# A decoder block in split float32 on one core: pool offsets, first gate/up weights, early form loads, two output queues

## The chip, the cores and the metric

The kernel runs on one core of one Trainium2 chip. The metric is the time of one execution in device microseconds (us), the median of repeated runs. A profile is one further execution with the hardware profiler on; its own time is given beside its span, since the two differ a little. PE is TensorE, DVE is VectorE, ACT is ScalarE, POOL is GpSimd, SP is SyncE; PEld is the load of the stationary operand on TensorE.

## The reference, cut to what matters

One decoder layer over 512 tokens of width 2048, everything in float32:

```
h   = RMSNorm(x)
[qA|kA|vA|qB|kB|vB|gA|gB] = h @ W_in
yA  = sliding-window attention (16 query heads, 4 key heads, window 128, sinks) @ W_branch_a
yB  = stick-breaking attention (16 heads, strictly causal) @ W_branch_b
x   = x + (sigmoid(gA) * yA + sigmoid(gB) * yB) @ W_out
x   = x + (silu(gate) * up) @ W_down      with [gate|up] = RMSNorm(x) @ W_ffn_in, 5632 wide
out = RMSNorm_final(x)
```

## The kernel before

**Products.** A float32 product is made of three passes over numbers that are rounded to the engine's fast 32-bit type: each operand is split in a high and a low part, and high*high, high*low and low*high are added in PSUM. Weights come in pieces of 128x1024: SP issues the load, ACT writes the high part (`whi`, line 153), DVE the low part (`wlo`, line 154). There are three buffers each of `raw`, `whi` and `wlo`, and the class `Weights` splits at most three pieces ahead of their use (`AHEAD`, line 128; `fill`, line 161). The list `todo` holds what is to be split; a callable in it stands for a piece of the feed-forward part, and `fill` stops at one as long as the pool `fp` doesn't exist.

**Stages.** First the input projection (lines 336 to 360 and 451 to 453), with both attentions worked off in between as pieces (`later`, `gap`); then the two branch projections, whose moving operands are `yh` and `yl`; then W_out (`rows`, lines 848 to 860; stationary operands `mh`, `ml`); then gate/up; then down.

**Gate/up and down.** Both use seven products in place of eight for a 2x2 block of sub-matrices (Strassen's scheme in Winograd's form): `p1` to `p7`, each on a sum of input quarters (a *form*, made by `make_forms`, lines 279 to 304) and a sum of weight quarters (`plan_group`, lines 210 to 246). One product step takes one pair of weight pieces with two forms and is 12 matmuls of 128x512 (`product`, lines 248 to 259). In these stages the form is the stationary operand (`fx`) and the weights (`whi`, `wlo`) move. `steps` (lines 200 to 208) sets the order of the steps: two products run in a staggered way, the second two steps behind the first, and at equal place the first one is ahead. There are 11 gate/up groups of 4 steps per product (each product reads the forms of pairs 0 to 7, two in a step), and 4 parts of down with 3, 3, 3 and 2 steps, each with two groups. In gate/up a `p5` piece is the sum of the `p1` piece (buffer `wx`) and a fresh load (`raw`); `p2` loads into the buffer `wz` that `p7` held.

**Forms between the stages.** Gate/up writes its results as forms to HBM (line 990, on POOL's queue); `load_forms` (lines 1012 to 1027) brings them back for down, on the same queue, together with the residual `x2`. Before the change it is called when the last gate/up group has been recorded. Even pairs land in pool `fp`, odd ones in pool `tp`. A DMA on POOL's queue that has to wait for a free tile holds up all that stand behind it.

**The end.** `finish` (line 1029) scales four tiles of 128 tokens by their root mean square, two column blocks on DVE and two on ACT, and SP issues the 16 stores of 256 KB (line 1039). The square root needs a table load on ACT.

**Order.** Instructions are recorded in the order of the code, and a scheduler then orders each engine's queue by its own model of times; dependencies through tiles and pools become waits.

**Places in SBUF.** From the left come the constants (`cp`), the weight buffers (`wp`) and 47 tiles of 2048 bytes (`tp`); from the right a pad of 24 numbers, 32 tiles of 2048 bytes (`ep`: `fh`, `fl`, `mh`, `ml`) and some constants (`ca`). Where `ep` and `ca` were, gate/up opens `fp` (21 tiles of 2048 bytes for `fx`, four each of 4096 bytes for `wx` and `wz`). In the program as built all tiles of `wp` and `tp` begin 512 bytes past a multiple of 2048 (`tp` at bytes 55,808 to 150,016 of a partition), and all of `ep` and `fp` begin 1920 bytes past one (`ep` at 163,712 to 227,200, `fp` from 153,472). `yh` and `yl` lie in `tp`; of the forms in gate/up pairs 0 to 4 lie in `tp` and 5 to 7 in `fp`.

## Time and profile before

| | us |
|---|---|
| median of 3 runs (2547.82 to 2552.52) | 2548.81 |
| the profiled execution's own time | 2547.38 |
| its span, first to last instruction | 2545.4 |

The page of the profile gives the busy time of each engine and the span in 40 slices (63.6 us each); the answers of the trace give single waits, single instructions with their start, and busy time by stretches. A matmul's duration in the trace is longer than the distance to the next one, since matmuls overlap in the array: how fast the engine goes is read from the starts, or from the number of matmuls in a stretch without a gap.

### The profile page before, as it was taken

Reading aid. Unit: us, or ns where it says so; the run is one execution under the profiler, and the core shown is the slowest. Engines: PE = TensorE matmul, PEld = TensorE weight load, DVE = VectorE, ACT = ScalarE, POOL = GpSimd, SP = SyncE. Lnnn points to the kernel's source line nnn. Section 1 sums busy time; section 2 is a strip of 40 time slices with the busy share of each in tenths; the row PEclk is TensorE's granted clock in tenths of the full one; section 3 lists DMA queues with packets and bytes.
Section 4 is the critical chain, followed back from the end, with each engine's and each line's share of the span. In section 5 each row is a group of like instructions: output and inputs, shape, how many; then the busy total and the mean of one; then the engine's idle time right before and its main releaser. Section 6 shows DMA issues by size and latency. Waiting matters only on the chain.

```text
span 2545.4 us, 33168 instructions
## 1 busy us (share of the span) xinstructions
PE 2502.8 (98%) x11529; PEld 2065.6 (81%) x11529; DVE 1980.7 (78%) x3457; ACT 1377.4 (54%) x2626; POOL 251.4 (10%) x482
## 2 busy tenths in 40 slices
PE   9999999999999999999999999999999999999997
PEld 8888878888887788888788888888888877888886
DVE  5688888888769644375788788888888877888888
ACT  6567777667657533265554555544555544333335
POOL 0000001111101000000010011100111024302100
PEclk9999999999999999999999999999999999999999
DMA  5232333333323644344456655566555689958652
GB/s 174 91 100 92 100 108 100 96 96 104 109 89 97 201 147 149 128 162 133 148 168 193 181 180 180 171 186 183 182 173 182 188 259 324 351 159 272 183 184 88
DMA packets 256295, 407.99 MB, mean 160 GB/s; under 512 B 16480, under 2 KB 103552, under 8 KB 256128
## 3 DMA queue, kind: packets, MB, share of 16 engines
q1 hardware_dynamic: 202096, 304.13, 38.5%
q0 software_dynamic: 46912, 89.15, 11.3%
q10 hardware_dynamic: 7120, 12.61, 1.3%
q8 instruction: 90, 1.47, 0.2%
q14 instruction: 77, 0.63, 0.1%
HBM read 344.48 MB, written 61.34 MB: 159 GB/s over the span
## 4 chain that ended last, share of the span: by engine, by line
PE 63%; issue 2%; ACT 1%; POOL 0%; DVE 0%; DMA 0%; ACTq 0%; POOLq 0%; DVEq 0%
PE mm L256 9%; PE mm L258 9%; PE mm L257 9%; PE at L256 7%; PE at L258 7%; PE at L257 7%; PE mm L341 3%; PE mm L342 3%; PE mm L340 3%; PE mm L856 1%; PE mm L857 1%; PE mm L858 1%; PE at L856 1%; PE at L858 1%; PE at L857 1%
## 5 line engine op out<-in xcount | busy, mean ns | idle before, releaser
L153 ACT CAST whi<-wx 128x1024 fp32r<-128x1024 f32 x264 | 277.2, 1050 | 333.5 <-PE at L258 150.5
L257 PE MATMUL mm<-wlo,fx 128*128 128x512 f32 x1056 | 417.3, 395 | 0.5 <-DVE wlo L154 0.5
L258 PE MATMUL mm<-whi,fx 128*128 128x512 f32 x1056 | 415.5, 393 | 0.0
L154 DVE TENSOR_TENSOR wlo<-wx,whi 128x1024 fp32r<-128x1024 f32 x264 | 322.6, 1223 | 112.4 <-ACT whi L153 110.5
L154 DVE TENSOR_TENSOR wlo<-raw,whi 128x1024 fp32r<-128x1024 f32 (+1 forms) x201 | 244.1, 1215 | 185.9 <-ACT whi L153 184.5
L256 PE MATMUL mm<-whi,fx 128*128 128x512 f32 x1056 | 375.7, 396 | 10.6 <-DMA fx<-f1p 5.5
L153 ACT CAST whi<-wz 128x1024 fp32r<-128x1024 f32 x198 | 207.8, 1050 | 283.0 <-PE mm L258 144.4
L342 PE MATMUL mm<-fh,wlo 128*128 128x512 f32 x896 | 354.9, 396 | 1.5 <-DVE wlo L154 1.5
L340 PE MATMUL mm<-fh,whi 128*128 128x512 f32 x896 | 354.8, 396 | 0.0
L341 PE MATMUL mm<-fl,whi 128*128 128x512 f32 x896 | 354.5, 396 | 0.0
L153 ACT CAST whi<-raw 128x1024 fp32r<-128x1024 f32 (+1 forms) x201 | 209.7, 1044 | 220.0 <-PE mm L341 131.2
L258 PE MATMUL at<-whi,fx 128*128 128x512 f32 x792 | 311.3, 393 | 0.0
L257 PE MATMUL at<-wlo,fx 128*128 128x512 f32 x792 | 310.8, 392 | 0.0
L593 ACT COPY turned<-z 32x128 f32<-32x128 f32 (+3 forms) x888 | 242.5, 273 | 106.0 <-DVE z L753 58.0
L154 DVE TENSOR_TENSOR wlo<-wz,whi 128x1024 fp32r<-128x1024 f32 x198 | 240.2, 1221 | 53.8 <-ACT whi L153 53.6
L256 PE MATMUL at<-whi,fx 128*128 128x512 f32 x792 | 279.8, 394 | 0.7 <-ACT whi L153 0.7
L256 PEld LDWEIGHTS mm<-whi,fx 128*128 128x128 f32 x1056 | 199.1, 189 | 53.9 <-DMA fx<-f1p 5.7
L257 PEld LDWEIGHTS mm<-wlo,fx 128*128 128x128 f32 x1056 | 199.5, 189 | 45.2 <-DVE wlo L154 1.7
L258 PEld LDWEIGHTS mm<-whi,fx 128*128 128x128 f32 x1056 | 199.5, 189 | 43.1
L342 PEld LDWEIGHTS mm<-fh,wlo 128*128 128x128 f32 x896 | 169.3, 189 | 42.2 <-DVE wlo L154 2.8
L341 PEld LDWEIGHTS mm<-fl,whi 128*128 128x128 f32 x896 | 169.5, 189 | 37.5
L340 PEld LDWEIGHTS mm<-fh,whi 128*128 128x128 f32 x896 | 169.2, 189 | 36.5
(254 smaller groups left out, 4177.8 us busy)
## 6 DMA issues: line engine op xcount, KB each, us to landing
raw<-in_w_in_dram SPq DMA_DIRECT2D x135, 512.0 KB, 3.6
raw<-in_w_ffn_in_dram SPq DMA_DIRECT2D x88, 512.0 KB, 3.7
wz<-in_w_ffn_in_dram SPq DMA_DIRECT2D x88, 512.0 KB, 4.4
wx<-in_w_ffn_in_dram SPq DMA_DIRECT2D x44, 512.0 KB, 4.4
raw<-in_w_ffn_down_dram SPq DMA_DIRECT2D x44, 512.0 KB, 4.2
wz<-in_w_ffn_down_dram SPq DMA_DIRECT2D x44, 512.0 KB, 5.0
raw<-in_w_out_dram SPq DMA_DIRECT2D x32, 512.0 KB, 3.6
wx<-in_w_ffn_down_dram SPq DMA_DIRECT2D x22, 512.0 KB, 5.5
```

What stands on the lines that cost most here:

```text
L153: nc.scalar.copy(hi[:, :n], raw[:, :n])
L154: nc.vector.tensor_tensor(out=lo[:, :n], in0=raw[:, :n], in1=f(hi[:, :n]), op=ALU.subtract)
L256: mm(banks[t], lhsT=hi, rhs=wh[:, kk, :], start=one, stop=False, skip_group_check=True)
L257: mm(banks[t], lhsT=hi, rhs=wl[:, kk, :], start=False, stop=False, skip_group_check=True)
L258: mm(banks[t], lhsT=lo, rhs=wh[:, kk, :], start=False, stop=end, skip_group_check=True)
L340: mm(b, lhsT=wh[:, kk, c], rhs=hi[k], start=(k == 0), stop=False)
L341: mm(b, lhsT=wh[:, kk, c], rhs=lo[k], start=False, stop=False)
L342: mm(b, lhsT=wl[:, kk, c], rhs=hi[k], start=False, stop=(k == nk - 1))
L593: copy(t4[c * Q : (c + 1) * Q, :, r], z4[r * Q : (r + 1) * Q, :, c])
L856: mm(banks[t], lhsT=hi[k][:, c], rhs=wh[:, kk, :], start=(k == 0), stop=False)
L857: mm(banks[t], lhsT=hi[k][:, c], rhs=wl[:, kk, :], start=False, stop=False)
L858: mm(banks[t], lhsT=lo[k][:, c], rhs=wh[:, kk, :], start=False, stop=(k == nk - 1))
```

## The change

Eight edits:

1. The pad at the right end grows from 24 to 376 numbers (96 to 1504 bytes). In the program as built all tiles of `ep`, `ca` and `fp` then begin 512 bytes past a multiple of 2048, as those of `wp` and `tp` do (`ep` at 162,304 to 225,792).
2. `plan_group` gets a flag `first` for the first gate/up group: its first two `p1` pieces are loaded into `raw`, its later `p5` pieces and its `p7` pieces use `wx` in place of `raw`. Its first three steps may be split before `fp` exists (`held`).
3. `steps` puts the second product's step ahead of the first's at equal place, in all groups of gate/up and down.
4. The second norm's instructions (`norm2`) are recorded behind the latest cast of weights.
5. `load_forms` becomes a generator; in the last gate/up group it is called on for two form names after `p6` and for two more after `p7`, and the rest after the group.
6. A square root of one column into the pad is recorded ahead of the last part of down.
7. Of the 16 output stores the 8 of odd column blocks go to POOL's queue.
8. The memset of the pad covers 8 columns.

```
--- before.py
+++ after.py
@@ -69,7 +69,7 @@
     tp = ctx.enter_context(tc.tile_pool(name="tp", bufs=47))
     early = ctx.enter_context(ExitStack())
     pad = ctx.enter_context(tc.tile_pool(name="pad", bufs=1, side="right"))
-    unused = pad.tile([P, 24], F32, tag="pad", name="pad")
+    unused = pad.tile([P, 376], F32, tag="pad", name="pad")
     ep = early.enter_context(tc.tile_pool(name="ep", bufs=32, side="right"))
     ca = early.enter_context(tc.tile_pool(name="ca", bufs=1, side="right"))
     ps = ctx.enter_context(tc.tile_pool(name="ps", bufs=4, space=bass.MemoryType.PSUM))
@@ -111,7 +111,7 @@
 
     ident = const("ident", P)
     make_identity(nc, ident)
-    nc.gpsimd.memset(unused, 0.0)
+    nc.gpsimd.memset(unused[:, :8], 0.0)
     ones = const("ones", P)
     nc.vector.memset(ones, 1.0)
 
@@ -135,8 +135,8 @@
             self.todo.append((w, k0, nk, c0, ncol))
 
         def split(self):
-            if callable(self.todo[0]):
-                self.ready.append(self.todo.popleft()())
+            if callable(self.todo[0][0]):
+                self.ready.append(self.todo.popleft()[0]())
                 return
             w, k0, nk, c0, ncol = self.todo.popleft()
             raw = wp.tile([P, 1024], F32, tag="raw", name=uid("raw"))
@@ -150,7 +150,7 @@
         def parts(self, raw, nk=2, n=1024):
             hi = wp.tile([P, 1024], F32R, tag="whi", name=uid("whi"))
             lo = wp.tile([P, 1024], F32R, tag="wlo", name=uid("wlo"))
-            nc.scalar.copy(hi[:, :n], raw[:, :n])
+            self.cast = nc.scalar.copy(hi[:, :n], raw[:, :n])
             nc.vector.tensor_tensor(out=lo[:, :n], in0=raw[:, :n], in1=f(hi[:, :n]), op=ALU.subtract)
             return (
                 hi[:, :n].rearrange("p (k c) -> p k c", k=nk),
@@ -158,8 +158,11 @@
                 nk,
             )
 
+        def held(self, item, early):
+            return callable(item) and not early and fp is None
+
         def fill(self):
-            while self.todo and len(self.ready) <= self.AHEAD and not (callable(self.todo[0]) and fp is None):
+            while self.todo and len(self.ready) <= self.AHEAD and not self.held(*self.todo[0][:2]):
                 self.split()
 
         def next(self):
@@ -202,12 +205,12 @@
         res = []
         for names in ORDER:
             for i in range(nq + 2 * (len(names) - 1)):
-                for e, name in enumerate(names):
+                for e, name in reversed(list(enumerate(names))):
                     if 0 <= i - 2 * e < nq:
                         res.append((name, i - 2 * e))
         return res
 
-    def plan_group(w, k0, nq, cols):
+    def plan_group(w, k0, nq, cols, first=False):
 
         xt, zt = [None] * nq, [None] * nq
 
@@ -228,22 +231,22 @@
 
         def item(name, j):
             if name == "p1":
-                xt[j] = load("wx", j, 0, 0)
+                xt[j] = load("raw" if first and j < 2 else "wx", j, 0, 0)
             elif name == "p5":
-                plus(xt[j], load("raw", j, 0, 1))
+                plus(xt[j], load("wx" if first and j else "raw", j, 0, 1))
             elif name == "p6":
                 zt[j] = load("wz", j, 1, 1)
                 plus(xt[j], zt[j])
             elif name == "p7":
-                plus(zt[j], load("raw", j, 0, 1))
+                plus(zt[j], load("wx" if first else "raw", j, 0, 1))
             elif name == "p2":
                 zt[j] = load("wz", j, 1, 0)
             elif name == "p4":
                 plus(xt[j], zt[j])
             return W.parts(zt[j] if name in ("p3", "p7", "p2") else xt[j])
 
-        for name, j in steps(nq):
-            W.todo.append(lambda name=name, j=j: item(name, j))
+        for i, (name, j) in enumerate(steps(nq)):
+            W.todo.append((lambda name=name, j=j: item(name, j), first and i < 3))
 
     def product(forms, banks, first, last, chunk=None, tiles=(0, 1)):
 
@@ -307,7 +310,7 @@
     NPAIR = KF // 2
     DOWN_PARTS = (3, 3, 3, 2)
     for g in range(NPAIR // 2):
-        plan_group(w_fi, 0, 4, (g * T, DFF + g * T))
+        plan_group(w_fi, 0, 4, (g * T, DFF + g * T), g == 0)
     k0 = 0
     for nq in DOWN_PARTS:
         for n in (0, 2):
@@ -917,8 +920,9 @@
     inv2 = const("inv2", NT)
 
     def norm2():
-        nc.vector.tensor_reduce(out=inv2, in_=ss2.rearrange("p (t c) -> p t c", t=NT), axis=AX.X, op=ALU.add)
-        rsqrt_mean(inv2, inv2, NT, [small(s, NT) for s in ("rv", "rr", "rq")])
+        with tc.issue_after(W.cast.ins):
+            nc.vector.tensor_reduce(out=inv2, in_=ss2.rearrange("p (t c) -> p t c", t=NT), axis=AX.X, op=ALU.add)
+            rsqrt_mean(inv2, inv2, NT, [small(s, NT) for s in ("rv", "rr", "rq")])
 
     late = [make_forms(xs2[2 * p], xs2[2 * p + 1], lambda name, p=p: form_slot(p, name)) for p in (5, 6, 7)]
     for _ in range(2):
@@ -935,8 +939,16 @@
         {name: dp.tile([P, T], F32R, tag=f"f{p}{name}", name=f"f{p}{name}") for name in FORMS} for p in range(NPAIR)
     ]
 
-    def gate_up(g):
+    def gate_up(g, loads=None):
         st = {}
+
+        def and_load(fn, n):
+            def both(b):
+                fn(b)
+                for _ in range(n if loads else 0):
+                    next(loads)
+
+            return both
 
         def copies(key):
             def fn(b):
@@ -991,11 +1003,7 @@
                 if len(res) in (2, 4):
                     return
 
-        group(4, xforms, {"p1": copies("a"), "p5": copies("c"), "p6": copies("t"), "p3": p3, "p7": p7, "p2": p2, "p4": p4})
-
-    pace[0] = 1.0
-    for g in range(NPAIR // 2):
-        gate_up(g)
+        group(4, xforms, {"p1": copies("a"), "p5": copies("c"), "p6": and_load(copies("t"), 2), "p3": p3, "p7": and_load(p7, 2), "p2": p2, "p4": p4})
 
 
     x2 = [[None] * 4 for _ in range(NT)]
@@ -1010,6 +1018,7 @@
     FIRST_READ = {"p1": (0, 0), "p5": (1, 1), "p6": (1, 0), "p4": (0, 1)}
 
     def load_forms(p0, np):
+
         res = [{} for _ in range(np)]
         for name in FORMS:
             if p0 == 0 and name in FIRST_READ:
@@ -1020,11 +1029,17 @@
                 else:
                     res[i][name] = slot("fx", F32R)
                 nc.gpsimd.dma_start(out=res[i][name], in_=form_d[p0 + i][name])
+            yield res
         if p0 == 0:
             for name in FIRST_READ:
                 n, half = FIRST_READ[name]
                 load_x2(n + 2, half)
-        return res
+        yield res
+
+    pace[0] = 1.0
+    loads = load_forms(0, 2 * DOWN_PARTS[0])
+    for g in range(NPAIR // 2):
+        gate_up(g, loads if g == NPAIR // 2 - 1 else None)
 
     def finish(t):
 
@@ -1036,7 +1051,8 @@
                 nc.scalar.activation(out=x2[t][m], in_=x2[t][m], func=AF.Copy, scale=inv)
             else:
                 nc.vector.tensor_scalar(out=x2[t][m], in0=x2[t][m], scalar1=inv, scalar2=None, op0=ALU.mult)
-            nc.sync.dma_start(out=out[t * P : (t + 1) * P, m * T : (m + 1) * T], in_=x2[t][m])
+            queue = nc.gpsimd if m % 2 else nc.sync
+            queue.dma_start(out=out[t * P : (t + 1) * P, m * T : (m + 1) * T], in_=x2[t][m])
 
     def down(nq, forms, n, last):
         def into(half, col, op, done=False, end=False):
@@ -1072,8 +1088,10 @@
     p0 = 0
     for part, nq in enumerate(DOWN_PARTS):
         last = part == len(DOWN_PARTS) - 1
-        dforms = load_forms(p0, 2 * nq)
+        for dforms in loads:
+            pass
         if last:
+            nc.scalar.activation(out=unused[:, 8:9], in_=inv2[:, :1], func=AF.Sqrt)
             for n in range(4):
                 gf[n] = slot("gf")
                 nc.sync.dma_start(out=gf[n], in_=norm_final_g[n * T : (n + 1) * T].partition_broadcast(P))
@@ -1082,6 +1100,8 @@
         while pieces:
             pieces.popleft()[1]()
         p0 += 2 * nq
+        if not last:
+            loads = load_forms(p0, 2 * DOWN_PARTS[part + 1])
 
 
 _INS = [
```

On POOL's queue, before, around the first load of an odd pair's `p1` form (`f1p_12391`; the numbers 12387 to 12390 are the names `p3`, `p7`, `p2` and `p4` of pair 0, `x` is the residual):

```order
L1022 DMA fx_19554<-f2p_12403 128x512
L1022 DMA fx_19558<-f4p_12417 128x512
L1022 DMA fx_19566<-f0p_12390 128x512
L1022 DMA fx_19570<-f2p_12404 128x512
L1022 DMA fx_19574<-f4p_12418 128x512
L1008 DMA x_3172_19478<-x_00_10804 128x512
L1008 DMA x_3173_19480<-x_10_10808 128x512
L1022 DMA fx_19484<-f1p_12391 128x512
```

The same place on POOL's queue after the change (`f1p_12392` is the `p1` form of pair 1, `f0p_12387` the `p6` form of pair 0):

```order
L1002 DMA f19p_12523<-fo_19145 128x512
L1002 DMA f19p_12524<-fo_19149 128x512
L1031 DMA fx_19398<-f0p_12387 128x512
L1031 DMA fx_19402<-f2p_12401 128x512
L1031 DMA fx_19406<-f4p_12415 128x512
L1016 DMA x_3130_19208<-x_00_10804 128x512
L1016 DMA x_3131_19210<-x_10_10808 128x512
L1031 DMA fx_19214<-f1p_12392 128x512
```

The load of the odd pair stood behind the even pairs' loads of all seven names, `p4` last; now it stands behind those of `p1`, `p5` and `p6` alone.

On ACT at the start of gate/up, before (`turned` are the last four transposed blocks, `whi_12299` is the first weight piece of gate/up):

```order
L885 ACTIVATE turned_12336<-at_12331,gcol 128x512
L885 ACTIVATE turned_12343<-at_12338,gcol 128x512
L885 ACTIVATE turned_12350<-at_12345,gcol 128x512
L885 ACTIVATE turned_12357<-at_12352,gcol 128x512
L366 ACT_TABLE_LOAD
L366 ACTIVATE rr_12839<-rv_12838 128x4
L288 CAST fx_12363<-turned_12336 128x256
L153 CAST whi_12299<-wx_12297 128x1024
```

On ACT after the change, from the last two pieces of W_out (`whi_12186`, `whi_12216`) on:

```order
L153 CAST whi_12186<-raw_12184 128x1024
L153 CAST whi_12216<-raw_12214 128x1024
L153 CAST whi_12246<-raw_12244 128x1024
L153 CAST whi_12276<-raw_12274 128x1024
L867 ACTIVATE j_12317,ss_10820<-x_1831_11929 128x512
L867 ACTIVATE j_12321,ss_10820<-x_1832_11932 128x512
L153 CAST whi_12312<-raw_12244 128x1024
```

The casts of the first gate/up pieces now stand ahead of the squares and of the transposed blocks, and the table load has moved from here to 35 rows behind the last `turned`.

On TensorE at the same place after the change (`whi_12246` is the first gate/up piece, `x` a block to be transposed):

```order
L861 MATMUL at_11944<-whi_12216,ml_10801 128x512
L259 MATMUL mm_12540<-whi_12246,fx_11233 128x512
L260 MATMUL mm_12540<-wlo_12247,fx_11233 128x512
L261 MATMUL mm_12540<-whi_12246,fx_11233 128x512
L259 MATMUL mm_12541<-whi_12246,fx_11233 128x512
```

These matmuls of gate/up stood behind the 16 transposes of `x`; now 14 of them stand between W_out's last matmul and the first transpose, and two more among the transposes.

The square root of edit 6 on ACT after the change, in the first gate/up group (`rr` is the second norm's root, `pad` that of edit 6):

```order
L369 ACT_TABLE_LOAD
L369 ACTIVATE rr_12840<-rv_12839 128x4
L153 CAST whi_12848<-wz_12797 128x1024
L957 COPY t_12864<-mm_12540 128x512
L957 COPY t_12865<-mm_12541 128x512
L153 CAST whi_12871<-wz_12680 128x1024
L1094 ACTIVATE pad<-inv_12360 128x1
```

It is recorded at the last part of down, but needs only `inv2`, and the scheduler has moved it up to here; ahead of the last root of `finish` the table load stands where it stood.

## Rows read from the trace of the kernel before

**Rows 1.** The page: busy time of TensorE, and DVE's busy tenths in 40 slices.

```profile
PE 2502.8 (98%) x11529; PEld 2065.6 (81%) x11529; DVE 1980.7 (78%) x3457; ACT 1377.4 (54%) x2626; POOL 251.4 (10%) x482
...
DVE  5688888888769644375788788888888877888888
```

**Rows 2.** TensorE's waits: who was waited for; us in total, times, longest.

```profile
PE mm L256 <- DMA fx<-f1p: 5.5, 1, 5.5
PE mm L256 <- ACT whi L153: 5.1, 1, 5.1
```

**Rows 3.** Two stretches: length, busy us (xcount) of each engine, clock, DMA share, GB/s.

```profile
870.00:1030.00 160.00, 160.00 (x708) 132.53 (x707) 75.18 (x116) 59.17 (x76) 0.00 (x0) 1.00 0.46 152
1045.00:1205.00 160.00, 160.00 (x690) 129.72 (x689) 94.11 (x252) 85.83 (x196) 6.64 (x12) 1.00 0.44 140
```

**Rows 4.** TensorE's timeline in the last gate/up group's p4: start, us, instruction.

```profile
2088.57 0.39 PE L256 MATMUL mm<-whi,fx 128*128 128x512 f32 x1
...
2089.70 0.39 PE L258 MATMUL mm<-whi,fx 128*128 128x512 f32 x1
...
2094.05 0.40 PE L257 MATMUL mm<-wlo,fx 128*128 128x512 f32 x1
...
2095.69 0.39 PE L258 MATMUL mm<-whi,fx 128*128 128x512 f32 x1
```

**Rows 5.** TensorE's timeline at the start of gate/up; idle before in brackets.

```profile
1216.51 1.93 PE L109 MATMUL at<-ident,x 128*128 128x128 f32 x16
1223.54 1.22 PE L256 MATMUL mm<-whi,fx 128*128 128x512 f32 x2 [5.11 <-ACT whi L153]
1225.27 0.79 PE L257 MATMUL mm<-wlo,fx 128*128 128x512 f32 x1 [0.51 <-DVE wlo L154]
```

**Rows 6.** ACT's timeline at the same place.

```profile
1218.31 2.42 ACT L885 ACTIVATE turned<-at,gcol 128x512 f32<-128x512 f32 x4
1220.75 1.28 ACT L366 ACT_TABLE_LOAD   x1
```

**Rows 7.** Timelines of POOL and TensorE at the start of down.

```profile
2096.38 0.54 POOL L1022 DMA_DIRECT2D fx<-f4p  x1 [0.86 <-PE mm L258]
2096.91 1.09 POOL L1008 DMA_DIRECT2D x<-x  x2
2098.00 0.55 POOL L1022 DMA_DIRECT2D fx<-f1p  x1
...
2103.77 0.79 PE L256 MATMUL mm<-whi,fx 128*128 128x512 f32 x1 [5.49 <-DMA fx<-f1p]
```

**Rows 8.** Two stretches behind these waits, columns as in rows 3.

```profile
1222.90:1229.90 7.00, 5.85 (x13) 4.17 (x14) 7.00 (x18) 5.24 (x12) 0.00 (x0) 0.51 1.05 394
2103.70:2107.20 3.50, 3.43 (x8) 2.76 (x9) 0.00 (x0) 0.43 (x1) 2.62 (x5) 0.51 1.09 389
```

**Rows 9.** Groups of matmuls by line and operands, with their count.

```profile
L257 PE MATMUL mm<-wlo,fx 128*128 128x512 f32 x1056 | 417.3, 395 | 0.5 <-DVE wlo L154 0.5
L342 PE MATMUL mm<-fh,wlo 128*128 128x512 f32 x896 | 354.9, 396 | 1.5 <-DVE wlo L154 1.5
L257 PE MATMUL at<-wlo,fx 128*128 128x512 f32 x792 | 310.8, 392 | 0.0
...
L356 PE MATMUL mm<-whi,fh 128*128 128x256 f32 x320 | 90.0, 282 | 0.0
```

**Rows 10.** The end: SP's timeline, and GB/s in 40 slices of 2500 to 2546.

```profile
2531.41 9.25 SPq L1039 DMA_DIRECT2D out_dram<-x  x16
...
GB/s 0 0 0 0 0 14 0 0 0 0 0 0 0 0 0 0 0 0 0 0 0 0 0 0 0 0 0 0 379 401 403 401 394 408 404 406 406 53 0 7
```

**Rows 11.** Timelines of DVE and ACT in gate/up: p7's last split, p4's sum, p2's cast.

```profile
1583.96 1.22 DVE L154 TENSOR_TENSOR wlo<-wz,whi 128x1024 fp32r<-128x1024 f32 x1
...
1589.86 1.22 DVE L227 TENSOR_TENSOR wx<-wx,wz 128x1024 f32<-128x1024 f32 x1 [0.84 <-DMA wz<-in_w_ffn_in_dram]
...
1591.03 1.05 ACT L153 CAST whi<-wz 128x1024 fp32r<-128x1024 f32 x1 [1.68 <-PE mm L258]
```


## What the change does to the time

> **What bounds the kernel now.** I read the page's busy times first, then TensorE's waits, then its speed where it waits for nobody. TensorE is busy for 2502.8 us of the span [rows 1], so nothing but less matmul time, or one of the few gaps, can shorten the kernel. Its two longest waits are 5.5 us at the start of down, for the form `f1p`, and 5.1 us at the start of gate/up, for the first weight piece [rows 2]. Speed is the larger matter. From 870 to 1030 us all matmuls are those of the branch projections, with both operands in `tp` and `wp`: 708 in 160 us, 226.0 ns each. From 1045 to 1205 us all are those of W_out, whose stationary operands `mh`, `ml` lie in `ep`: 690 in 160 us, 231.9 ns each [rows 3]. No gap stands in either stretch and the clock is 1.00 in both. Nor is it the stage: in one product of gate/up, `p4` of the last group, five distances between starts from 2088.57 to 2089.70 make 226 ns, where the forms are those of pairs 0 to 4 in `tp`; seven from 2094.05 to 2095.69 make 234 ns, where they are those of pairs 5 to 7 in `fp` [rows 4]. So a matmul that touches a tile 1920 bytes past a multiple of 2048, together with one 512 bytes past, is about 6 ns slower, whether that tile moves or is stationary.
>
> **The pad: 5.9 ns on some 6,100 matmuls.** The new pad puts every tile at 512 past a multiple of 2048. Which matmuls does that concern? Line 342 reads `fh` 896 times, and lines 340 and 341 are its two sisters: 2688 [rows 9]; the first projection block (lines 451 to 453) has 96 more. W_out has 4 column blocks x 16 rows x 4 token tiles x 3 = 768. Gate/up has 11 x 7 x 4 x 12 = 3696 and down 2 x 7 x 11 x 12 = 1848, together 5544, which is three times the 1056 + 792 of line 257 [rows 9]. Three eighths of gate/up's forms lie in `fp` (1386) and half of down's (924); and since the next stationary operand is loaded under the running matmul, the last matmul ahead of each run counts too, 77 in gate/up and 154 in down. The sum is 2784 + 768 + 1386 + 924 + 231 = 6093. By the difference of [rows 3], 231.9 - 226.0 = 5.9 ns, this is 35.9 us. The 960 matmuls of 256 columns (line 356 and its two sisters, 320 each [rows 9]) have no like at the equal offset; between 0 and 5.9 ns they bring 0 to 5.7 us, and I take 0, as no row shows a gain at this width. All this comes off the path only where TensorE is the bound. DVE is at eight or nine tenths in most slices [rows 1], and in one slice of the attention (the thirteenth) at nine or more; there attention's pieces, not TensorE, may set the pace. I take off 3 us for it: **-33 us**, with ends 0 and -41.6.
>
> [...]
>
> **The start of gate/up.** TensorE's transposes end W_out at 1218.4; the first matmul of gate/up comes at 1223.54, after 5.11 us, and DVE's half costs 0.51 more [rows 5]. ACT was not waiting for the weights: it had the last transposed blocks (2.42 us) and the table load of the second norm (1.28 us) ahead of the cast [rows 6]. Behind the wait the clock is at 0.51 from 1222.9 to 1229.9 [rows 8], the lower of its two levels, after TensorE had stood still: 6.4 us of work from 1223.54 on took twice its time, a loss of 3.2. With the change the first pieces are split under W_out's last matmuls, and 14 matmuls (3.2 us) go ahead of the transposes. The forms of pairs 6 and 7 need the transposes and ACT's 2.42 us; 34 more matmuls (7.7 us) stand ahead of their first use, so they are covered, unless ACT, with the casts now in between, comes late. Of 5.1 + 0.5 + 3.2 = 8.8 I keep 1.0 for that: **-7.8 us**, ends 0 and -8.8.
>
> **The start of down.** `f1p` was asked for at 2098.00, at once behind `f4p` of name `p4` (2096.38) and two blocks of `x2`, because that even load waited for a tile that TensorE gave free at the very end; TensorE then stood for 5.49 us [rows 7]. The clock behind it is at 0.51 for 3.5 us [rows 8], a loss of 1.7. In the new order `f1p` stands behind the even loads of `p6`, whose tiles are free when `p6` of the last group is through, with three to four products of 11 us each still to come. So the wait goes with its slow clock. The loads take the same queue and the same bytes, only earlier; the stores of forms behind them on POOL wait a little longer, and who reads these is the last part of down. **-7.2 us**, ends 0 and -7.2.
>
> **The rest.** The stores at the end are 16 issues from 2531.41 on, and the DMA engines then move 380 to 408 GB/s without a pause [rows 10]: 4.2 MB at 400 GB/s are 10.5 us whichever queue asks. Two queues save issue time that isn't on the path; POOL takes about 0.54 us per issue [rows 7] against SP's 9.25/16 = 0.58 [rows 10]. I take 0, ends -1 and +1.5 for POOL's last store. The square root of edit 6 does not do what its place in the code suggests: the scheduler has put it into the first gate/up group, and the table load stands at the end as before: 0. The smaller memset, the moved norm: 0, covered by the whole of the first group.
>
> **The sum.** -33 - 7.8 - 7.2 = -48. The profiled execution took 2547.38 and the median is 2548.81, 1.4 more. 2548.8 - 48 = 2500.8: I say **2501 us**.
>
> **Rival 1: the place, not the offset.** Every tile at 1920 also lies at byte 153,472 or above; no row separates the two. If high places are slow by themselves, the pad brings 0 and only the two starts are left: 2548.8 - 15 = 2534. Against it: the same 6 ns appears for a moving and for a stationary operand, and for tiles spread over 70 KB. Chance 0.15.
>
> **Rival 2: another engine takes half.** With TensorE 1 to 2% faster, pieces of attention, forms or DVE's sums come late at many places. For it speak DVE's 8s and 9s [rows 1]; against it, that DVE had only 94 of 160 us to do in [rows 3] and that TensorE's list of waits is so short [rows 2]. Half of -33: 2548.8 - 16.5 - 15 = 2517. Chance 0.09.
>
> **Rival 3: slower, by `p2`'s loads.** A `p2` load waits until `p7`'s split has read the buffer. Before, that split ended at 1585.18, the load was there at 1589.86, 4.7 us later, and the cast began at 1591.03 [rows 11], set by TensorE's release. The new order of steps puts the first and the last `p2` piece of a gate/up group one step (12 x 0.226 = 2.7 us) nearer to `p7`. The cast wanted at 1588.3 then starts at 1589.9, is done with DVE's half at about 1592.3, and its first matmul is due two steps after 1588.3, at 1593.7: 1.4 us to spare. Where loads take over 4.7 + 1.4 = 6.1 us, TensorE waits twice in each of 11 groups. At 7.1 us this is 22 us, and with the pad bringing nothing 2548.8 - 15 + 22 = 2556; it passes the time before from loads of 6.8 us on, if rival 1 holds as well. Chance 0.03.
>
> **How the numbers follow.** The forecast has 0.70, the rivals 0.15, 0.09 and 0.03, and 0.03 is left for what I don't see. The forecast's own range is 2490 (all ends: -41.6 - 8.8 - 7.2 - 1 = -58.6) to 2512 (pad -24, starts -13). It holds too little, so the range reaches over rivals 2 and 1 to 2535. A measurement of this kernel can tell 0.2%, 5 us, from no change. Faster: forecast, rivals 1 and 2 but for a hundredth, 0.93. Same, 0.03: the pad brings nothing and a start keeps its wait. Slower, 0.04: rival 3 and a part of the rest.
>
> **What will show it.** In the new trace W_out's stretch should hold as many matmuls in 160 us as that of the branches, 706 to 708, and the starts in `p4` should be 0.226 to 0.228 us apart throughout. TensorE's waits should hold neither `f1p` nor the first `whi`, and no stretch of half clock should stand at either start. I am wrong if W_out stays near 690; if DVE or ACT appears in TensorE's waits in gate/up; or if the span behind the last matmul grows by over 1.5 us.

## The result: 33 us faster, 14 short of the forecast

| | before | after |
|---|---|---|
| median of 4 runs (range), us | 2548.32 (2547.35 to 2552.52) | 2515.00 (2514.04 to 2517.31) |
| the profiled execution / its span, us | 2547.38 / 2545.4 | 2515.71 / 2513.6 |

The ratio is 0.9867, 95% interval 0.985 to 0.9885. The forecast was 2501. The page after, with the same lines as [rows 1]:

```profile
PE 2472.4 (98%) x11529; PEld 2063.3 (82%) x11529; DVE 1977.8 (79%) x3457; ACT 1377.9 (55%) x2627; POOL 256.4 (10%) x490
...
DVE  5688888988769644376788888888888878888888
```

TensorE has 30.4 us less to do for the same 11529 matmuls. The stretches of [rows 3] (length, busy us and count of PE, PEld, DVE, ACT, POOL, clock, DMA share, GB/s) now hold the same number of matmuls. In TensorE's timeline (start, us, instruction) the starts in `p4` of the last group [rows 4] are 0.227 us apart, (2069.91 - 2068.32) / 7:

```profile
870.00:1030.00 160.00, 160.00 (x707) 132.48 (x707) 75.22 (x117) 59.32 (x76) 0.00 (x0) 1.00 0.44 145
1045.00:1205.00 160.00, 160.00 (x707) 132.48 (x707) 97.73 (x257) 87.50 (x201) 7.80 (x15) 1.00 0.46 147
```

```profile
2068.32 0.39 PE L260 MATMUL mm<-wlo,fx 128*128 128x512 f32 x1
...
2069.91 0.39 PE L261 MATMUL mm<-whi,fx 128*128 128x512 f32 x1
```

TensorE's waits (us in total, times, longest), the longest of those that came or grew. Both rows of [rows 2] are gone:

```profile
...
PE at L661 <- ACT ph L601: 4.2, 1, 4.2
PE at L260 <- DVE wlo L154: 4.1, 3, 1.8
PE mm L345 <- DVE wlo L154: 3.7, 3, 1.8
PE at L259 <- ACT whi L153: 2.6, 2, 2.0
...
PE mm L260 <- DVE wlo L154: 1.1, 2, 0.9
```

Lengths of the stages, from the start of one stage's first matmul to the next one's, in us; the first row runs from the span's start, the last one from the last matmul's start to the span's end. The columns add up to the spans. Two kernels of the experiments stand beside them: the pad alone, and the last one below.

| stage | before | after | pad alone | last kernel |
|---|---|---|---|---|
| input projection and attentions | 863.90 | 856.24 | 856.43 | 857.47 |
| branches, W_out, to gate/up's first matmul | 359.64 | 348.16 | 355.23 | 348.16 |
| gate/up, first group | 82.18 | 86.84 | 81.01 | 78.93 |
| gate/up, nine groups | 710.70 | 703.74 | 703.49 | 703.32 |
| gate/up, last group | 79.51 | 80.89 | 79.86 | 78.16 |
| down, first part | 125.20 | 117.87 | 123.80 | 115.90 |
| down, three parts | 309.73 | 304.90 | 304.86 | 304.87 |
| end | 14.51 | 14.98 | 14.54 | 14.02 |

So the start of gate/up comes earlier, but its first group takes 4.7 us more; the start of down is shorter, but the group ahead of it is longer; and the attentions give 7.7 where the pad's term had 16.4. Kernels with the same code in a stage can differ there. The run with all stores on SP (below) has the code of the change up to the end, but its first gate/up group took 85.65 us and its last 82.36. After TensorE's wait in the first group the granted clock was at its lower level, 0.50, for 3.4 us, and for 6.8 with the change; after that in the last group it was so for 3.4 us, and not at all with the change. The attentions differ in the same way, by 1.1 us behind the wait for `ph`. So a difference of under 1.5 us in one of these stages, or of under 2 in the medians, shows no effect by itself.

### The profile page after: what moved, and what is told of

Read it like the earlier page. It is cut to its first block, busy times and chain, and to the rows that moved or that the text cites. A ratio compares the mean times of both kernels' runs of the same rounds, so it can differ in the third digit from the quotient of the medians.

```text
span 2513.6 us, 33228 instructions
## 1 busy us (share of the span) xinstructions
PE 2472.4 (98%) x11529; PEld 2063.3 (82%) x11529; DVE 1977.8 (79%) x3457; ACT 1377.9 (55%) x2627; POOL 256.4 (10%) x490
## 4 chain that ended last, share of the span: by engine, by line
PE 50%; issue 12%; POOL 2%; DVE 2%; DMA 1%; ACT 0%; POOLq 0%; DVEq 0%
PE mm L261 7%; PE mm L260 7%; PE mm L259 6%; PE at L260 5%; PE at L261 5%; PE at L259 5%; PE mm L345 3%; PE mm L343 3%; PE mm L344 3%; POOL fx L1031 2%; PE at L860 1%; PE mm L861 1%; PE mm L860 1%; PE at L861 1%; PE at L859 1%
## 5 line engine op out<-in xcount | busy, mean ns | idle before, releaser
L153 ACT CAST whi<-wx 128x1024 fp32r<-128x1024 f32 x256 | 269.6, 1053 | 306.5 <-PE mm L261 132.0
L261 PE MATMUL mm<-whi,fx 128*128 128x512 f32 x1056 | 411.9, 390 | 0.0
L154 DVE TENSOR_TENSOR wlo<-raw,whi 128x1024 fp32r<-128x1024 f32 (+1 forms) x209 | 253.7, 1215 | 186.1 <-ACT whi L153 184.4
L154 DVE TENSOR_TENSOR wlo<-wx,whi 128x1024 fp32r<-128x1024 f32 x256 | 312.6, 1222 | 80.5 <-ACT whi L153 80.1
L259 PE MATMUL mm<-whi,fx 128*128 128x512 f32 x1056 | 369.4, 390 | 0.4 <-ACT whi L153 0.4
L153 ACT CAST whi<-raw 128x1024 fp32r<-128x1024 f32 (+1 forms) x209 | 218.2, 1046 | 222.9 <-PE mm L344 126.8
```

Source lines behind the costliest of these rows:

```text
L153: self.cast = nc.scalar.copy(hi[:, :n], raw[:, :n])
L154: nc.vector.tensor_tensor(out=lo[:, :n], in0=raw[:, :n], in1=f(hi[:, :n]), op=ALU.subtract)
L259: mm(banks[t], lhsT=hi, rhs=wh[:, kk, :], start=one, stop=False, skip_group_check=True)
L261: mm(banks[t], lhsT=lo, rhs=wh[:, kk, :], start=False, stop=end, skip_group_check=True)
```

## Experiments

Some stage lengths in the expectations are not those of the traces: the attentions' gain is 7.7 and not 8.3, and from the last matmul's start to the end it is 14.98 and 14.51 us, not 4.56 and 3.46, and 14.54 and 14.86 with the pad alone and the left shift, not 3.0 and 3.9.

### The pad: offset, place or value

Pad alone (before, with edits 1 and 8):

```
-    unused = pad.tile([P, 24], F32, tag="pad", name="pad")
+    unused = pad.tile([P, 376], F32, tag="pad", name="pad")
-    nc.gpsimd.memset(unused, 0.0)
+    nc.gpsimd.memset(unused[:, :8], 0.0)
```

> The kernel before with edits 1 and 8 alone (pad of 376 numbers, memset of 8 columns). Theory A (equal offsets make TensorE faster; 6093 matmuls x 5.9 ns = 36 us, part of it given back as waits on DVE and ACT): W_out's stretch holds 706 to 708 matmuls in 160 us, and the time falls by 24 to 33 us, since the trace after the change shows input projection with attention only 8.3 us shorter where 16.4 were due. Rival (the place in SBUF, not the offset): 690 in 160 us and the time of before, within 3 us; the trace after the change speaks against it already, its W_out tiles still lie above byte 162,000.

Left shift (before, its pad kept):

```
     make_identity(nc, ident)
+    shift = const("shift", 352)
+    nc.gpsimd.memset(shift[:, :8], 0.0)
```

> The kernel before with its pad of 24, and 1408 bytes of constants added at the left, so that the tiles of wp and tp begin 1920 bytes past a multiple of 2048, as those of ep and fp do; ep and fp stay where they were. Theory A (equal offsets): W_out at 706 to 708 matmuls in 160 us, the time as with the pad alone, 24 to 33 us below before. Rival place (tiles at high bytes are slow): W_out at 690, no gain. Rival value (512 is a good offset by itself and 1920 a bad one): W_out and the branches at 690, and the other matmuls slower too, some 4,500 x 5.9 ns = 26 us above before.

Pad of 248 (before, `pad.tile([P, 248], ...)`):

> The kernel before with a pad of 248 numbers: ep and fp begin 1024 bytes past a multiple of 2048, wp and tp 512. Theory A in its strict form (the offsets must be equal modulo 2048): W_out near 690 in 160 us, 0 to -3 us. Rival form (equal modulo 512 is enough): 706 to 708 and 24 to 33 us less, as with the pad alone. Anything between says that the distance has a size of its own.

Measured, against 2548.64 before: pad alone 2522.2, ratio 0.9895 (0.988 to 0.9909); left shift 2521.14, 0.9891 (0.9876 to 0.9906); pad of 248 2523.92, 0.9901 (0.9886 to 0.9916). W_out's stretch in the three:

```profile
1045.00:1205.00 160.00, 160.00 (x709) 132.49 (x708) 93.82 (x254) 85.19 (x199) 7.72 (x14) 1.00 0.43 135
```

```profile
1045.00:1205.00 160.00, 160.00 (x711) 132.55 (x710) 94.15 (x254) 85.53 (x200) 7.94 (x15) 1.00 0.42 136
```

```profile
1045.00:1205.00 160.00, 160.00 (x708) 132.48 (x707) 93.22 (x253) 84.59 (x197) 7.18 (x13) 1.00 0.42 135
```

All three have the fast rate, where before had 690 [rows 3]. In the left shift `ep` and `fp` stay exactly where they were, so the place (rival 1) falls; and everything lies at 1920 there, so 1920 is not bad by itself (711 matmuls, 225.0 ns each). With the pad of 248 the offsets are 512 and 1024: a distance of 512 is as good as none in this stretch (708 matmuls against 709 and 711), which I had not expected. A distance of 1408 costs some 6 ns a matmul (231.9 against 226.0 ns [rows 3]), and taking it away with the pad alone brings 26.4 us; other distances weren't tried. Why a distance of 1408 is slow no run shows.

### All edits but the pad, and each of three edits undone

```
-    unused = pad.tile([P, 376], F32, tag="pad", name="pad")
+    unused = pad.tile([P, 24], F32, tag="pad", name="pad")
```

> The changed kernel with the pad back at 24 numbers, so all edits but the first. By the terms of the prediction (starts of gate/up and down, -7.8 and -7.2): 15 us below before, 2533. By the trace after the change (starts net -1.6 and -3.2, tail +1.1): some 4 us below before, 2544. Rival: the starts gain their 15 as long as TensorE is slow, and lose it again to DVE only with the pad; then 2533 here.

Measured: 2541.40, ratio 0.9971 (0.9962 to 0.9981), 7.2 less than before. With the pad's 26.4 that makes 33.6; the whole gave 33.3. So the parts simply add, and neither reaches its term (33 and 15). The stages of this run: first matmul of gate/up 7.0 us nearer, the first group 4.1 longer, the last 1.5 longer, the first part of down 6.2 shorter. The losses are there with the slow TensorE too.

Undone, each in the changed kernel: the early loads, the flag `first`, the reversed steps.

```
-        gate_up(g, loads if g == NPAIR // 2 - 1 else None)
+        gate_up(g)
```

> The changed kernel without edit 5's early loads (no group is handed the loads; they all stand behind the last gate/up group, as before). By the prediction's term: 7.2 us above the changed kernel, with TensorE's wait for f1p back at 5 to 6 us and the last group unchanged. By the traces (the last group 1.4 us longer with the change, 1.2 longer than its ten sisters already with the pad alone): the wait comes back, but the last group gets 1 to 1.5 us shorter, net 4 to 6 us above. Rival: the last group's loss belongs to edit 3's order; then it stays as long as in the changed kernel and the whole is 7 above.

```
-        plan_group(w_fi, 0, 4, (g * T, DFF + g * T), g == 0)
+        plan_group(w_fi, 0, 4, (g * T, DFF + g * T))
```

> The changed kernel without edit 2 (the flag first is off: the first pieces wait for fp as before). By the prediction's term: 7.8 us above the changed kernel. By the traces (stretch up to the first matmul of gate/up 7.0 shorter by edits 2 to 4 in both settings of the pad, first group 4.1 to 5.8 longer): 1 to 3 us above, and the first group back near 81 us. Rival: the first group's loss is edit 3's order and stays without edit 2; then 7 above.

```
-                for e, name in reversed(list(enumerate(names))):
+                for e, name in enumerate(names):
```

> The changed kernel without edit 3 (at equal place the first product's step is ahead again). If the order of steps costs or brings nothing by itself: every gate/up group but the first and last within 0.2 us of the changed kernel's 78.15, the time within 2 us. If edit 3 makes the loss in the first group (its second product wants a sum of weights one step earlier): the first group 2 to 5 us shorter and the time as much below. If edit 3 is what lets the first group start early: the wait for the first pieces comes back, 2 to 5 us above.

| | median, us | ratio to before (95%) | first group | last group | down, first part |
|---|---|---|---|---|---|
| changed kernel | 2515.00 | 0.9867 (0.985 to 0.9885) | 86.84 | 80.89 | 117.87 |
| no early loads | 2518.18 | 0.9882 (0.9867 to 0.9896) | 85.65 | 78.77 | 122.21 |
| no `first` | 2516.94 | 0.9878 (0.9861 to 0.9894) | 82.35 | 80.37 | 117.38 |
| old steps | 2518.26 | 0.9881 (0.9866 to 0.9896) | 88.96 | 81.33 | 117.28 |

Without early loads the wait for `f1p` is back, at 3.6 us, and the last group is 2.1 us shorter: the edit is worth 2.2 by these two stages and 3.2 by the medians, and my 4 to 6 was too much. Without `first` gate/up starts 5.6 us later and its first group is 4.5 shorter: 1.1 by the stages and 1.9 by the medians, hardly to be told from nothing. So each loss belongs to its own edit, and the reversed order is not its cause: without it the first group is 2.1 us longer still, and groups two to ten stay as they are (most at 78.17 against 78.15). None of the three cases that I had written down for this run came. Edit 3, which my sum had at nothing, brings 2 to 3 us at this one place.

### The first gate/up group: DVE's queue

After the change, at the start of gate/up: the timelines of PE and of DVE (idle before in brackets), and seven us as a stretch with the columns above:

```profile
1204.17 0.39 PE L861 MATMUL at<-whi,ml 128*128 128x512 f32 x1
1204.40 0.39 PE L259 MATMUL mm<-whi,fx 128*128 128x512 f32 x1
...
1225.05 0.50 PE L260 MATMUL at<-wlo,fx 128*128 128x512 f32 x1 [0.71 <-DVE wlo L154]
...
1231.81 0.80 PE L260 MATMUL at<-wlo,fx 128*128 128x512 f32 x1 [1.80 <-DVE wlo L154]
```

```profile
1208.45 1.23 DVE L154 TENSOR_TENSOR wlo<-wx,whi 128x1024 fp32r<-128x1024 f32 x1 [0.79 <-ACT whi L153]
...
1227.40 2.09 DVE L292 TENSOR_TENSOR fx<-turned,fx 128x256 fp32r<-128x256 f32 x6
1229.41 1.21 DVE L230 TENSOR_TENSOR wx<-wx,wz 128x1024 f32<-128x1024 f32 x1
1230.54 1.21 DVE L154 TENSOR_TENSOR wlo<-wx,whi 128x1024 fp32r<-128x1024 f32 x1
1231.68 2.34 DVE L154 TENSOR_TENSOR wlo<-raw,whi 128x1024 fp32r<-128x1024 f32 x2
```

```profile
1230.00:1237.00 7.00, 5.20 (x13) 4.17 (x13) 5.16 (x5) 1.27 (x4) 0.00 (x0) 0.57 0.04 13
```

W_out runs into gate/up without a gap, as forecast. But DVE works from 1208.45 to 1235 without a pause. Six halves of forms of pairs 5 to 7 for `p2` and `p4` (L292 at 1227.40), which TensorE reads some 14 product steps later at the earliest, stand ahead of a `wlo` for which it waits 1.80 us; after these waits the granted clock is 0.57 on the mean from 1230 to 1237, and 0.50 from 1231 to 1237. The test asks for these pieces later:

```
-    for _ in range(3):
-        for gen in late:
-            later(lambda gen=gen: next(gen), 1)
-    for gen in late:
-        later(lambda gen=gen: [None for _ in gen], 1)
-    later(norm2, 1)
+    for n in range(3):
+        for i, gen in enumerate(late):
+            later(lambda gen=gen: next(gen), 3 + 4 * n + i)
+    for i, gen in enumerate(late):
+        later(lambda gen=gen: [None for _ in gen], 15 + i)
+    later(norm2, 18)
```

> The changed kernel with the pieces that make the forms of pairs 5 to 7 for p6, p3, p7, p2 and p4 asked for later in the first gate/up group (at steps 3 to 17 in place of 1 to 12; the second norm behind them). If the first group's loss is DVE's backlog (27 us of work without a gap from 1208 us on, of which these pieces are some 30 instructions of 0.34 to 0.41 us, about 11 us): TensorE's waits for wlo and whi there go or shrink to under 2 us in sum, the first group falls from 85.7 or 86.8 to between 80 and 83 us, and the time by 3 to 6 us. Rival (the first group is late because its weights land late or because buffers are short): the group stays above 85 us and the time within 1 us.

Measured: 2508.76, ratio 0.9845 (0.9832 to 0.9859). The first group falls from 86.84 to 78.96 us, more than expected. The same 35 us with the change and in this run:

```profile
1205.00:1240.00 35.00, 30.68 (x127) 23.70 (x126) 30.80 (x53) 21.58 (x43) 0.98 (x2) 0.90 0.41 142
```

```profile
1205.00:1240.00 35.00, 34.62 (x161) 28.45 (x160) 33.72 (x56) 24.56 (x47) 1.29 (x3) 1.00 0.47 163
```

161 matmuls in place of 127, at full clock, with DVE just as full: it was the order of DVE's work, not its amount. The rival falls. The last group became 3.8 us longer at once (84.73), with a wait for `whi` of 3.6 and 6.8 us at the lower clock behind it.

### The last gate/up group: form loads against weights

Where the change asks for forms early, `p2`'s weights are late (timeline of PE; DMA issues from 2030 to 2056 us with count, KB and median us to landing; two stretches with the DMA rate in the last column). With the change:

```profile
2047.75 0.73 PE L259 MATMUL at<-whi,fx 128*128 128x512 f32 x2 [1.96 <-ACT whi L153]
```

```profile
wz<-in_w_ffn_in_dram SPq DMA_DIRECT2D x4, 512.0 KB, 8.6
```

```profile
2040.00:2045.00 5.00, 5.00 (x24) 4.14 (x23) 1.19 (x2) 0.00 (x0) 1.95 (x4) 1.00 1.10 362
2045.00:2050.00 5.00, 2.82 (x12) 1.72 (x11) 3.42 (x3) 2.38 (x3) 2.18 (x4) 1.00 1.13 399
```

Without the early loads the same issues read:

```profile
wz<-in_w_ffn_in_dram SPq DMA_DIRECT2D x4, 512.0 KB, 4.7
```

The wait is for the first two of the four, which land after 8.8 and 9.5 us with the change and after 6.0 and 6.5 without the early loads; there TensorE doesn't wait. That fits rival 3's bound of some 6.1 us for a `p2` load, but its cause is another: with the old order of steps the last group is as long (81.33). First I halved the early loads:

```
-"p6": and_load(copies("t"), 2), "p3": p3, "p7": and_load(p7, 2),
+"p6": and_load(copies("t"), 1), "p3": p3, "p7": and_load(p7, 1),
```

> The changed kernel with the early loads halved: one form name asked for after p6 and one after p7, in place of two and two. If the last group's loss comes from form loads that share the DMA engines with the weights of its p2: the wait for whi there (2.0 us) shrinks to under 0.8, the last group falls from 80.9 or 82.4 to 79 to 80 us, the first part of down stays at 117 to 118, the time falls by 1 to 2 us. Rival (any early load costs the last group the same): the last group stays above 80.5. Rival (the names left behind are late at the start of down): a wait for a form of p5 or p6 there of 1 to 3 us.

Measured: 2512.71, 0.986 (0.9846 to 0.9873); the last group 80.72. The first rival holds: ten issues are still made within 7 us of `p6`'s end, and the first two `p2` loads still land after 8.6 and 9.5 us; only the first part of down gained (115.94). Then the sum of what was known, with all stores on SP (next section):

> The two edits of the runs before it in one (forms of pairs 5 to 7 later, early loads halved), and all output stores on SP. If the three losses are separate: the sum of their gains against the changed kernel, 3 to 6 at the first group, 1 to 2 at the last, 1.9 at the end by the stage lengths of the run with SP alone: 6 to 10 us less, 2505 to 2509. If they are not, or the stores' gain is a matter of chance: 2510 or more.

Measured: 2507.34, 0.9839 (0.9825 to 0.9852): first group 78.95, last group 83.06, end 13.94. Within the range, but the gain at the last group isn't in it. So the loads were moved in time, not in number: nothing behind `p6`, and four of the residual's blocks made to wait for the cast of a `p2` weight (`hold`, set in `and_load`, read in `load_x2`). Against the combined kernel:

```
-"p6": and_load(copies("t"), 1), "p3": p3, "p7": and_load(p7, 1),
+"p6": copies("t"), "p3": p3, "p7": and_load(p7, 2),
...
             self.cast = nc.scalar.copy(hi[:, :n], raw[:, :n])
+            self.hi, self.hold = hi, None
...
+                    W.hold = W.hi
                     next(loads)
+                    W.hold = None
...
             x2[t][n] = slot("x2")
+            if W.hold is not None:
+                nc.vector.tensor_copy(x2[t][n][:, :1], f(W.hold)[:, :1])
```

> As the combined run before it (later forms of pairs 5 to 7, all output stores on SP), but the early form loads stand elsewhere: none is asked for behind p6 of the last gate/up group; those of p1 and p5 stand on POOL's queue behind the even loads of p3 and the first of p7, some 12 us later, and two blocks of the residual wait for the cast of a p2 weight by a copy of one column. The last group's wait is for p2's weights, asked for at 2037.8 in the changed kernel and landing after 8.6 us there, 4.7 us without early loads. If the form loads asked for at the same moment make that difference: these weights land within 6 us again, the wait for whi goes, the last group falls from 83.1 (81 where no half clock follows) to 78.2 to 79.0, the time to 2502 to 2505. Rival (the loads are now late for the start of down): a wait for f1p or a p5 form of 1 to 4 us there, 2506 to 2509. Rival (the weights are late whatever stands on POOL's queue, because the group starts earlier now): no change, 2507.

Measured: 2502.99 (2502.41 to 2504.18), ratio 0.9823 (0.9809 to 0.9837). `p2`'s weights land after 4.3 us, the first two after 5.2 and 5.6; the last group takes 78.16, the first part of down 115.90, and from 1985 to 2200 us TensorE waits for nothing. This kernel beats both. Its page and its weights:

```profile
PE 2465.7 (99%) x11529; PEld 2060.8 (82%) x11529; DVE 1978.2 (79%) x3461; ACT 1377.7 (55%) x2627; POOL 251.2 (10%) x482
```

```profile
wz<-in_w_ffn_in_dram SPq DMA_DIRECT2D x4, 512.0 KB, 4.3
```

### The stores at the end

```
-            queue = nc.gpsimd if m % 2 else nc.sync
+            queue = nc.sync
```

> The changed kernel with all 16 output stores on SP again. If the second queue makes the longer end (4.56 us from the last matmul's start to the end, 3.46 before): the end back at 3.0 to 3.5 us, the time about 1 us below the changed kernel. If the end's length only depends on which kind of execution it is (3.0 with the pad alone, 3.9 with the left shift): between 3.0 and 4.5, no difference.

Measured: 2515.12, 0.9867 (0.9853 to 0.9882), the same median; but the end is 13.66 us in place of 14.98, and the stretch of the attentions behind the wait for `ph` was 1.1 us longer in this profile. The issues, first with the change, then in this run (timelines of SP and POOL; DMA issues with median us to landing):

```profile
2499.23 7.56 SPq L1055 DMA_DIRECT2D out_dram<-x  x8
...
2504.95 2.38 POOL L1055 DMA_DIRECT2D out_dram<-x  x4 [2.29 <-ACT x L1051]
```

```profile
out_dram<-x SPq DMA_DIRECT2D x8, 256.0 KB, 2.8
out_dram<-x POOLq DMA_DIRECT2D x8, 256.0 KB, 4.3
```

```profile
2499.75 9.25 SPq L1055 DMA_DIRECT2D out_dram<-x  x16
```

```profile
out_dram<-x SPq DMA_DIRECT2D x16, 256.0 KB, 2.7
```

In all seven kernels with two queues the end is 14.9 to 15.3, in the three that have edits 2 to 6 and SP alone 13.7 to 14.0. Edit 7 costs about 1.2 us. Why the end with SP alone was 14.5 to 14.9 without the other edits wasn't tried.

## Why the prediction was right, and why it was off

The direction and the range were right, the likeliest case was not. That 2515 lies by rival 2's 2517 is luck: rival 2 took half of the pad's 33 and kept both starts whole, while the pad lost 6.6 of its 33 and the other edits brought 7.2 where the starts had 15. Rival 2's mechanism, other engines that are late because TensorE is faster, fits the attentions alone; the first and the last gate/up group lose with the slow TensorE too (4.1 and 1.5 us in the run of all edits but the pad). Rival 3's late `p2` loads came in one group, and from the form loads, not from the order of steps.

- **The pad, -33.** It gave 26.4. The 5.9 ns of [rows 3] were right: W_out 4.4 us (768 x 5.9 = 4.5), gate/up 8.0 (1463 x 5.9 = 8.6), down 6.3 (1078 x 5.9 = 6.4), by the stage lengths of the pad alone. The step that failed is "I take off 3 us" for places where DVE is bound: the attentions gave 7.5 of 16.4 us, so 9 are lost there. The loss has places. Cut into 39 pieces of 96 matmuls, the projection has 24 pieces of 512 columns that got 0.4 to 0.6 us shorter, 12.2 together (13.6 by the 5.9 ns). Four got longer, by 3.3 us together where 2.3 were due the other way; they make the two stretches below, the same matmuls before and after (columns as in [rows 3]). Nine pieces of 256 columns, for which the prediction had a gain of 0 to 5.7 us, took 0.9 more. The first two pieces are mixed and hold the kernel's start. The pad alone, the left shift and the pad of 248 agree in this within 1.1 us.

```profile
310.17:363.38 53.21, 49.76 (x211) 40.03 (x210) 44.08 (x113) 40.68 (x103) 0.00 (x0) 0.97 0.29 90
779.78:840.54 60.76, 54.32 (x234) 42.73 (x232) 54.72 (x172) 45.67 (x136) 7.29 (x16) 0.97 0.30 95
```

```profile
306.10:361.81 55.71, 49.58 (x211) 39.59 (x210) 46.56 (x119) 41.54 (x106) 0.00 (x0) 0.97 0.28 86
771.79:833.34 61.55, 55.99 (x233) 44.75 (x232) 55.42 (x176) 46.42 (x139) 7.30 (x16) 0.92 0.29 94
```

In the first stretch TensorE waits 6.0 us in place of 3.4, for `ph`, a `wlo` and `pl`; in the second 5.6 in place of 6.4, but with a clock of 0.92 on the mean in place of 0.97. Before, the waits for `ph` and for `wlo` in the projection, which are 4.2 and 3.7 after (first fence of waits above), were:

```profile
PE at L658 <- ACT ph L598: 3.4, 1, 3.4
...
PE mm L342 <- DVE wlo L154: 1.5, 1, 1.5
```

With the slow TensorE (all edits but the pad) these stretches are within 0.8 us of before, so it is the faster TensorE that finds the others late; but no run took work from DVE or ACT there, and whether their order or their amount does it is not shown.

- **The start of gate/up, -7.8.** Gate/up's first matmul did come 7.1 us nearer beyond the pad's part (348.16 against 355.23). The first group gave 5.8 back (86.84 against 81.01): 1.3 net. The failed step is the cover: I asked only whether ACT comes late, and kept 1.0 for it. DVE had the same pieces to split, with the forms of pairs 5 to 7 it had 27 us of work in a row, and halves of forms that TensorE didn't need yet stood ahead of a `wlo` that TensorE waited for. With the forms later the first group is 2.1 us below the pad alone: 9.2 in all, more than the end of -8.8.
- **The start of down, -7.2.** `f1p`'s wait and its slow clock went, as forecast (5.9 us of the first part beyond the pad; the granted clock is 1.00 there now); the last group lost 1.0 more than with the pad alone: 4.9 net. The early loads alone carry 2 to 3 of it, by the run without them; what brings the rest wasn't tried. The failed step is "the same queue and the same bytes, only earlier". Earlier means together with `p2`'s weights, on another queue but the same DMA engines: from 2030 to 2056 the packets of POOL's queue took 63.6% and those of SP's 42.6% of the 16 engines' time, and from 2040 to 2050 the engines moved 362 to 399 GB/s. At a time when these weights have landed, the two places together gain 9.6 over the pad alone.
- **The rest, 0.** The end grew by 0.5, inside its end of +1.5: the bandwidth argument was right that two queues gain nothing (390 to 411 GB/s during the stores with two, 378 to 406 with SP alone), and POOL's stores land 1.5 us later (4.3 against 2.8). The square root of edit 6 took no table load from the end, as forecast: one still stands at 2495.26, 1.28 us; no run undoes edit 6. Edit 3 was worth 2 to 3 us, not 0.

One sign of being wrong, "if DVE or ACT appears in TensorE's waits in gate/up", was the right thing to watch; they stand there in the first and the last group. With the three losses taken back the kernel is at 2503, near the forecast's 2501, but not by its terms: the pad stays 7 short of its 33, and the two starts bring 9.2 and 9.6 where 7.8 and 7.2 were booked. What the sum had wrong in the changed kernel is that it booked the starts as if the work moved under cover had room there.

## What to carry to other kernels

When a step is moved to hide a wait, list what every engine and the DMA engines do in the place it moves to, not only the engine that was late. Here a transfer made earlier needed a moment in which nothing urgent was on the way, and when it was asked for decided more than how much: with half of the early loads the first two `p2` weights still landed after 8.6 and 9.5 us, with loads asked for later after 5.2 and 5.6. Where two stages run the same matmuls at different rates without a wait (here 231.9 and 226.0 ns [rows 3]), compare the offsets of the operands' tiles in SBUF.

## What the hardware showed that was not expected

- Matmuls of 128x512 whose operands lie 1408 bytes apart modulo 2048 took 231.9 ns (690 in 160 us); at 0 and at 512 bytes apart 225.0 to 226.3 (707 to 711), with the tiles at either offset. Those of 256 columns got no faster at equal offsets (0.9 us longer over 864 of them).
- Weight loads of 512 KB on SP's queue landed after 8.6 us in place of 4.7 (medians of four) when forms were loaded by POOL's queue at the same time.
- Stores of 256 KB landed after 4.3 us from POOL's queue and 2.8 from SP's, side by side.
